# Attention with the rows of the next pair of heads made in the units in front, and three smaller moves around it

## The chip, the cores and the metric

The kernel runs on one core of a Trainium2 chip. The metric is the device time of one execution in microseconds (us). A core has a matrix engine (PE, whose weight loads are listed apart as PEld), three engines for elementwise work (DVE, ACT and POOL), and queues from which DMA transfers are issued (SP, ACT and POOL have one each).

## The reference

Two transformer blocks on 512 tokens of width 1024, in fp32. The first block ends in a mixture of 8 experts, of which each token takes two. The second block is the one that the change touches:

```python
    hn = modulate(rms_norm(h, norm1_g), shift1, scale1)
    qa, ka, va, qb, kb, vb = split(hn @ w_in)
    # a heads (8): dilated windows over rms-normalised q and k, added up with softmax weights
    for window, dilation in DILATED_PATTERNS:
        o, l = dilated_window_attention(rms_norm(qa), rms_norm(ka), va, table_a, window, dilation)
    # b heads (4): softmax(q1 k1 + bias) - lam * softmax(q2 k2 + bias), times v, rms-normalised
    o_b = differential_attention(qb[0], qb[1], kb[0], kb[1], vb, table_b, lam)
    h = h + gate1 * (concatenate([o_a, o_b]) @ w_out)
    hn = modulate(rms_norm(h, norm2_g), shift2, scale2)
    u = depthwise_conv_centred(hn @ w_up, conv_w, conv_b)      # 3 taps over tokens
    val, gate = split(u)
    h = h + gate2 * ((silu(gate) * val) @ w_down)
```

## The kernel before

Tokens lie in four blocks of 128 (`tb`). A product in fp32 is made of three matmuls (`mm3`, L173): each operand is split by `part` into a high part (a CAST on ACT, L167) and a low part (a subtraction on DVE, L168). Sums go to a pool of 8 banks of PSUM, tag `mm`. A scheduler of the framework puts the instructions of each engine in order when the kernel is built; `issue_after` makes an instruction stand behind another on the same queue. `skewed(units, lags)` runs generators one behind the other, each a step at a time.

**Combine.** Behind the last expert its rows `yde` are written to memory (L1582, issued on ACT's queue). Eight gathers on POOL's queue (L2236) fetch each token's two rows back. Per token block DVE adds them to `xres` (L2243) and takes statistics; POOL makes the factors of a layer norm from them (`bnrs`, L1137 to L1139), ACT applies these (`rsq`, L1140), DVE multiplies (L2247) and POOL adds a row vector (L2248). An RMS norm follows: ACT's squares (L2055), POOL's `rms` and `rrs`, and `rdg` on DVE (L2060), a diagonal matrix by which PE turns `xres` into the features `hT` (L1164, then `u` on ACT and DVE, L1169 and L1171). `gate3` and `gate4` are vectors that a DMA of POOL's queue spreads over all partitions (`bcast`, L301, tile `bc`, 512 KB each); they are wanted behind `w_out` and at the end.

**w_in.** Six column chunks (`ch`); in each, four pieces of weights of 256 rows, and with a piece six matmuls for each of the four token blocks.

**Attention.** `heads` makes the rows of a pair of a heads, or of a b head: PE transposes (L1890), then for each half six steps on ACT and DVE: three activations (L1899 to L1901) and two scaled subtractions (L1902, L1903), into `apair` or `act`. `zload` loads a head's bias rows and splits them (`zh`, `zl`). A unit is a quarter of a head's queries (`qb` 0 to 3). Its steps, in the lags (0, 1, 2, 4, 6): prepare; scores (four matmuls, L1918); maximum, exponential (`asc`, L1927), reciprocal and scaling (L1949, or L1975 for b heads); four transposes of the probabilities (L1935) and a copy to `PT` (L1936); the products with the values (L1960) at the last quarter of a pair. All of `heads` and `zload` is done in the prepare step of `qb` 0.

**Convolution.** For each pair of 128 columns of `w_up`, a value and a gate product of 24 matmuls over all 512 tokens each, then the taps, silu and product.

## Time and profile before

| | |
|---|---|
| median of 3 runs | 3006.85 us (3003.61 to 3007.26) |
| profiled execution | 2995.27 us, its span 2993.5 us |
| mean granted clock of PE | 0.906 |
| busy, share of the span | PE 88%, PEld 67%, DVE 57%, ACT 45%, POOL 27% |
| from the last expert to the first w_in product | about 2198 to 2253.5 us |
| w_in / attention / convolution FFN | to about 2385 / to about 2559 / from 2626.6 us |

The profile is one execution, some 0.4% below the median of the timed runs. A granted clock of 1.0 is 2.4 GHz, 0.5 is 1.2 GHz. In the rows further down, times are us from the start of the span; "out<-in" are the program's tile names; what stands in brackets is how long the engine had stood idle before the instruction, and whose end released it.

### The profile page before, as it was taken

The numbers are of one execution on the slowest core, as the hardware profiler recorded it, in microseconds if no ns is written. First come the engines' busy times: TensorE is split into PE (matmuls) and PEld (weight loads), VectorE is DVE, ScalarE is ACT, GpSimd is POOL, SyncE is SP. The second block draws the span as 40 slices with busy tenths as digits, with TensorE's granted clock in tenths as the row PEclk, the third lists the DMA queues.
The fourth block names the chain that finished last, engine by engine and source line by source line (L and its number), as shares of the span: only waits on it lengthen the run. The fifth ranks groups of instructions, "written<-read, shape, count | busy, mean of one in ns | idle before, by whom it ended". The sixth has DMA issues, their size and how long they took to land. (4 is left out here: it accounts for less than half of the span.)

```text
span 2993.5 us, 48068 instructions
## 1 busy us (share of the span) xinstructions
PE 2645.0 (88%) x18864; PEld 1998.6 (67%) x18864; DVE 1717.4 (57%) x2529; ACT 1335.1 (45%) x2338; POOL 822.6 (27%) x905
## 2 busy tenths in 40 slices
PE   6878798898898867789997999999949999899999
PEld 3666577677676556678776666455638756778887
DVE  5875656656756547664456423456675468554545
ACT  5644545645645433225442322345543367442422
POOL 2363435534525312016653300000042100102120
PEclk7986888987987978999998999999979989999999
DMA  7572334544544547666632877777762212223231
GB/s 259 175 235 69 97 116 131 177 153 129 168 122 117 156 147 236 203 198 212 198 120 101 286 277 274 262 259 267 279 212 81 62 42 70 71 71 99 98 97 58
DMA packets 301824, 477.92 MB, mean 160 GB/s; under 512 B 47283, under 2 KB 176068, under 8 KB 294936
## 3 DMA queue, kind: packets, MB, share of 16 engines
q1 hardware_dynamic: 283896, 404.81, 41.1%
q0 software_dynamic: 10480, 60.31, 6.1%
q10 hardware_dynamic: 7216, 9.68, 1.0%
q8 instruction: 151, 2.47, 0.3%
q14 instruction: 81, 0.66, 0.1%
HBM read 419.34 MB, written 55.39 MB: 159 GB/s over the span
## 5 line engine op out<-in xcount | busy, mean ns | idle before, releaser
L168 DVE TENSOR_TENSOR wl<-w,wh 128x1024 fp32r<-128x1024 f32 (+2 forms) x400 | 478.9, 1208 | 612.2 <-ACT wh L167 608.2
L167 ACT CAST wh<-w 128x1024 fp32r<-128x1024 f32 (+2 forms) x400 | 382.6, 966 | 619.4 <-PE mm L173 425.8
L173 PE MATMUL mm<-act,wh 128*128 128x512 f32 (+1 forms) x1440 | 446.1, 392 | 28.7 <-ACT act L167 22.8
L173 PEld LDWEIGHTS mm<-act,wh 128*128 128x128 f32 x1440 | 273.3, 193 | 87.5 <-ACT act L167 23.8
L173 PE MATMUL mm<-wh,act 128*128 128x512 f32 x884 | 288.1, 398 | 7.2 <-ACT wh L167 3.9
L173 PE MATMUL mm<-act,wl 128*128 128x512 f32 (+1 forms) x720 | 280.8, 390 | 4.8 <-DVE wl L168 4.8
L173 PEld LDWEIGHTS mm<-wh,act 128*128 128x128 f32 x884 | 168.1, 191 | 51.6 <-ACT wh L167 6.1
L173 PE MATMUL mm<-wl,act 128*128 128x512 f32 x474 | 188.9, 399 | 0.1
L286 POOL TENSOR_TENSOR act<-act 128x512 f32<-128x512 f32 x96 | 144.0, 1500 | 156.2 <-ACT act L285 141.5
L301 POOL DMA_DIRECT2D bc<-gate x6 | 3.5, 591 | 605.7 <-DVEq L1739 508.4
L173 PEld LDWEIGHTS mm<-act,wl 128*128 128x128 f32 x720 | 138.4, 192 | 35.0 <-DVE wl L168 7.7
L799 DVE STREAM_TRANSPOSE XT<-T 128x512 f16<-128x512 f16 x120 | 84.6, 705 | 99.3 <-ACT T L797 99.2
L743 POOL TENSOR_TENSOR GA<-GA,masks 128x512 f32<-128x512 f32 (+1 forms) x96 | 99.8, 1050 | 103.8 <-ACT GA L742 100.6
L739 PE MATMUL gm<-kr,bk 64*128 64x128 f32 (+1 forms) x768 | 117.1, 331 | 3.5 <-DVE kk L645 1.7
L792 DVE TENSOR_TENSOR W<-pW,masks 128x512 f16<-128x512 f32 x120 | 81.7, 681 | 65.9 <-PE pW L790 62.0
L285 ACT ACTIVATE act<-act,cT 128x512 f32<-128x512 f32 x96 | 68.4, 724 | 112.1 <-DMA act<-in_w_ada_dram 111.8
L739 PEld LDWEIGHTS gm<-kr,bk 64*128 64x128 f32 x768 | 101.2, 230 | 24.2 <-ACT GA L742 8.6
L173 PE MATMUL mm<-wh,moxl 128*128 128x512 f32 (+1 forms) x336 | 113.5, 381 | 0.3 <-ACT wh L167 0.3
L850 POOL TENSOR_TENSOR SP<-S,pc 128x64 f32<-128x64 f32 x176 | 59.0, 353 | 195.0 <-DVE S L890 183.6
L173 PE MATMUL mm<-wh,moxh 128*128 128x512 f32 (+1 forms) x336 | 107.0, 388 | 5.4 <-ACT wh L167 5.3
L173 PEld LDWEIGHTS mm<-wl,act 128*128 128x128 f32 x474 | 90.8, 192 | 28.3 <-issue 4.9
L288 DVE SCALAR_TENSOR_TENSOR act<-act,cT 128x512 f32<-128x512 f32 x96 | 74.2, 773 | 57.8 <-DMA act<-in_ada_w_dram 56.8
(529 smaller groups left out, 6155.8 us busy)
## 6 DMA issues: line engine op xcount, KB each, us to landing
w<-in_moe_w_dram SPq DMA_DIRECT2D x136, 512.0 KB
w<-in_moe_w_dram SPq DMA_DIRECT2D x40, 1024.0 KB
w<-in_ffn_w_dram SPq DMA_DIRECT2D x32, 1024.0 KB
act<-in_ada_w_dram SPq DMA_DIRECT2D x96, 256.0 KB
act<-in_w_ada_dram SPq DMA_DIRECT2D x96, 256.0 KB
w<-in_moe_w_dram SPq DMA_DIRECT2D x64, 384.0 KB
w<-in_w_up_dram SPq DMA_DIRECT2D x22, 1024.0 KB
x<-xdk POOLq DMA_DIRECT2D x18, 1024.0 KB, 6.0
```

Of the source, the lines that this page charges most:

```text
L167: self.nc.scalar.copy(out=hi, in_=x)
L168: self.nc.vector.tensor_tensor(out=lo, in0=x, in1=hi.bitcast(F32), op=OP.subtract)
L173: self.nc.tensor.matmul(ps, x, y, start=start and i == 0, stop=stop and i == 2, skip_group_check=True)
L285: nc.scalar.activation(out=wt, in_=wt, func=AF.Copy, scale=c)
L286: nc.gpsimd.tensor_tensor(out=acc, in0=wt, in1=acc if kk else bias, op=OP.add)
L288: nc.vector.scalar_tensor_tensor(out=acc, in0=wt, scalar=c, in1=acc if kk else bias, op0=OP.mult, op1=OP.add)
L301: (eng or self.nc.gpsimd).dma_start(out=t, in_=row_ap.to_broadcast([128, D]))
L739: nc.tensor.matmul(pss[par][:, s2, d, :nc_], bkj(d, par, j), KR[d][PR(par), j::12, :][:, :nc_ // 64, :], start=True, stop=True)
L743: nc.gpsimd.tensor_tensor(out=out, in0=out, in1=gm, op=OP.mult)
L792: nc.vector.tensor_tensor(out=W16, in0=pW, in1=lmask[:, li, None].to_broadcast(sh), op=OP.mult)
L799: nc.vector.transpose(fl(XT), fl(T16))
L850: nc.gpsimd.tensor_tensor(out=SP[:, d], in0=S[:, d], in1=PC[d][:, j:j + 1].to_broadcast([128, 64]), op=OP.mult)
```

## The change

Gate3's broadcast is put behind the last gather (`taken`) on POOL's queue. In w_in, chunk 0 takes its first three pieces of weights together, a token block at a time (18 matmuls in a row), and has three buffers of split weights instead of two. `heads` becomes a generator that gives its two halves one at a time; those of pair i+1 are made in the prepare steps of `qb` 1 and 2 of the last head of pair i, and a head's bias rows at `qb` 3 of the head in front. The first block of the convolution makes its value and gate products in halves of 256 tokens, value and gate of the first half ahead of the second half.

```diff
-            k.wq = win.enter_context(tc.tile_pool(reuse_waits="tile", name="wqC", bufs=2))
+            k.wq = win.enter_context(tc.tile_pool(reuse_waits="tile", name="wqC", bufs=3))
...
                         w = k.part(raw[:, 2 * q2:2 * q2 + 2, :])
+                        ws.append(w)
+                        if not ch and len(ws) < 3:
+                            continue
+
                         for tb in range(4):
-                            for k2 in range(2):
-                                kk = q * 4 + q2 * 2 + k2
+                            for kk in range(0 if len(ws) == 3 and not ch else 2 * len(ws) - 2, 2 * len(ws)):
+                                w, k2 = ws[kk // 2], kk % 2
                                 k.mm3(pss[tb], at(hT, ALL, kk, slice(tb * 128, (tb + 1) * 128)), at(w, ALL, k2), kk == 0, kk == KB - 1)
...
-        def heads(blk, hp):
+        def heads(blk, hp, out):
...
                 out.append((q, kh, kl, r))
-            return out
+                yield
...
+        order = [(0, hp) for hp in range(4)] + [(1, h) for h in range(4)]
+        coming = []
+
+        def start(i):
+            if i < len(order):
+                rowsets[order[i]] = []
+                coming.append(heads(*order[i], rowsets[order[i]]))
+
+        def prepare(i, h, qb, last):
+
+            if last and qb == 1:
+                start(i + 1)
+            if last and qb in (1, 2) and i + 1 < len(order):
+                next(coming[-1])
+            if qb == 3 and h < 11:
+                zs_[h + 1] = zload(h + 1)
+
+        start(0)
+        for _ in coming[0]:
+            pass
+        zs_[0] = zload(0)
 
         def unit_a(h, qb, st):
-            if qb == 0:
-                if h % 2 == 0:
-                    pairs[h // 2] = heads(0, h // 2)
-                st["hd"], st["z"] = pairs[h // 2][h % 2], zload(h)
-            yield
-            ps = scores(st["hd"], st["z"], qb)
+            prepare(h // 2, h, qb, h % 2 == 1)
+            yield
+            ps = scores(rowsets[0, h // 2][h % 2], zs_[h], qb)
...
         def unit_b(h, qb, st):
-            if qb == 0:
-                st["h1"], st["h2"] = heads(1, h)
-                st["z"] = zload(8 + h)
-            yield
-            pss = [scores(st[n_], st["z"], qb) for n_ in ("h1", "h2")]
+            prepare(4 + h, 8 + h, qb, True)
+            yield
+            pss = [scores(hd, zs_[8 + h], qb) for hd in rowsets[1, h]]
...
+        def products(ts, i, n=1):
+
+            ws = [k.part(t[:, :, i * 128:(i + 1) * 128]) for t in ts]
+            pss = [k.t(psp, [128, 512], tag="mm") for _ in ts]
+            for j in range(n):
+                cs = slice(j * NT // n, (j + 1) * NT // n)
+                for w, ps in zip(ws, pss):
+                    for kk in range(KB):
+                        k.mm3(ps[:, cs], at(w, ALL, kk), at(hT, ALL, kk, cs), kk == 0 and j == 0, kk == KB - 1 and j == n - 1)
+            return pss
...
-                    uv = conv(f + i, tv, i)
-                    ug = conv(22 + f + i, tg, i)
+                    if f + i:
+                        uv = conv(f + i, *products([tv], i))
+                        ug = conv(22 + f + i, *products([tg], i))
+                    else:
+
+                        pv, pg = products([tv, tg], i, 2)
+                        uv, ug = conv(f + i, pv), conv(22 + f + i, pg)
...
-                    nc.gpsimd.indirect_dma_start(out=got[c][:, tb, :], out_offset=None, in_=rows.yd,
+                    taken = nc.gpsimd.indirect_dma_start(out=got[c][:, tb, :], out_offset=None, in_=rows.yd,
...
-        gate3 = k.bcast(bc, k.gates["2"][0])
+        with tc.issue_after(taken.ins):
+            gate3 = k.bcast(bc, k.gates["2"][0])
```

On POOL, where the combine begins (`act_22171`, `act_22172` are the gathered rows, `bc_22383` is gate3, `bc_25357` gate4, `bnrs_22193` and `bnrs_22208` are the factors of token blocks 0 and 1), before (rows 652 to 656 are gathers like the two ahead of them):

```order
649 L301 DMA bc_25357<-gate_15617 128x1024
650 L2236 DMA act_22171<-yde,rt_rg 128x1024
651 L2236 DMA act_22172<-yde,rt_rg 128x1024
657 L2236 DMA act_22172<-yde,rt_rg 128x1024
658 L1137 TENSOR_SCALAR bnrs_22193<-bnag_22189 128x1
659 L1138 TENSOR_TENSOR bnrs_22193<-bnrs_22193,mhalf 128x1
660 L1139 TENSOR_TENSOR bnrs_22193<-bnrs_22193,bnnm_22191 128x1
661 L2248 TENSOR_TENSOR xres<-xres,bb_18774 128x1024
662 L1137 TENSOR_SCALAR bnrs_22208<-bnag_22204 128x1
663 L1138 TENSOR_TENSOR bnrs_22208<-bnrs_22208,mhalf 128x1
664 L1139 TENSOR_TENSOR bnrs_22208<-bnrs_22208,bnnm_22206 128x1
```

and now:

```order
654 L2269 DMA act_22171<-yde,rt_rg 128x1024
655 L2269 DMA act_22172<-yde,rt_rg 128x1024
656 L301 DMA bc_22383<-gate_15616 128x1024
657 L301 DMA bc_25357<-gate_15617 128x1024
658 L1137 TENSOR_SCALAR bnrs_22193<-bnag_22189 128x1
659 L1138 TENSOR_TENSOR bnrs_22193<-bnrs_22193,mhalf 128x1
660 L1139 TENSOR_TENSOR bnrs_22193<-bnrs_22193,bnnm_22191 128x1
661 L1137 TENSOR_SCALAR bnrs_22208<-bnag_22204 128x1
662 L1138 TENSOR_TENSOR bnrs_22208<-bnrs_22208,mhalf 128x1
663 L2281 TENSOR_TENSOR xres<-xres,bb_18774 128x1024
664 L1139 TENSOR_TENSOR bnrs_22208<-bnrs_22208,bnnm_22206 128x1
```

Both broadcasts stand behind the gathers now, ahead of the first `bnrs`; of block 1's three steps two have moved ahead of the add on `xres`.

On ACT, from the copy of the output of pair 0's products (`act_22387`) on, before (`apair` are the rows of a pair, `zh` a head's bias, `asc` the exponentials, `PT` the copies of transposed probabilities of the units that run):

```order
1800 L167 CAST act_22387<-mm_23580 128x512
1801 L1936 COPY PT_23554<-mm_23604 128x4x128
1802 L1936 COPY PT_23554<-mm_23623 128x4x128
1803 L1927 ACTIVATE asc_23662,asm_23663<-mm_23610,amx_23660 128x512
1804 L1899 ACTIVATE apair<-mm_23629,qncols 64x512
1805 L1900 ACTIVATE apair<-mm_23634,qncols 64x512
1806 L1901 ACTIVATE apair<-mm_23634,qncols 64x512
1807 L167 CAST zh_23734<-zr_23732 128x896
1808 L1936 COPY PT_23668<-mm_23669 128x4x128
1809 L1927 ACTIVATE asc_23682,asm_23683<-mm_23655,amx_23680 128x512
1810 L1936 COPY PT_23668<-mm_23688 128x4x128
1811 L1899 ACTIVATE apair<-mm_23629,qncols 64x512
```

and now, where the rows of the same pair (`apair<-mm_23561`, `mm_23566`) are made, up to that copy:

```order
1795 L1931 ACTIVATE asc_23548,asm_23549<-mm_23522,amx_23546 128x512
1796 L1931 ACTIVATE asc_23583,asm_23584<-mm_23541,amx_23581 128x512
1797 L1903 ACTIVATE apair<-mm_23561,qncols 64x512
1798 L1904 ACTIVATE apair<-mm_23566,qncols 64x512
1799 L1905 ACTIVATE apair<-mm_23566,qncols 64x512
1800 L1931 ACTIVATE asc_23618,asm_23619<-mm_23576,amx_23616 128x512
1801 L1903 ACTIVATE apair<-mm_23561,qncols 64x512
1802 L1904 ACTIVATE apair<-mm_23566,qncols 64x512
1803 L1905 ACTIVATE apair<-mm_23566,qncols 64x512
1804 L1940 COPY PT_23554<-mm_23555 128x4x128
1805 L1940 COPY PT_23554<-mm_23589 128x4x128
1806 L167 CAST act_22387<-mm_23595 128x512
```

These are the rows of pair 2. Its six activations stood behind the copy, in two groups with a bias between them; they now stand ahead of it, with one exponential between the groups, and the bias is elsewhere.

On PE, at the first products of the convolution, behind the last transposes (L1164), before (`mm_25377`, `mm_25410` are two sums over all 512 tokens):

```order
15329 L1164 MATMUL mm_25331<-rdg_25329,xres 128x128 x4
15330 L1164 MATMUL mm_25343<-rdg_25329,xres 128x128 x4
15331 L173 MATMUL mm_25377<-act_24961,wh_25378 128x512
15332 L173 MATMUL mm_25410<-act_24961,wh_25411 128x512
15333 L173 MATMUL mm_25447<-act_24961,wh_25448 128x512
15334 L173 MATMUL mm_25377<-act_24962,wh_25378 128x512
15335 L173 MATMUL mm_25377<-act_24961,wl_25379 128x512
```

and now (`mm_25385` is the value's sum, `mm_25386` the gate's):

```order
15311 L1164 MATMUL mm_25331<-rdg_25329,xres 128x128 x4
15312 L1164 MATMUL mm_25343<-rdg_25329,xres 128x128 x4
15313 L173 MATMUL mm_25385<-act_24961,wh_25377 128x256
15314 L173 MATMUL mm_25386<-act_24961,wh_25381 128x256
15315 L173 MATMUL mm_25385<-act_24962,wh_25377 128x256
15316 L173 MATMUL mm_25385<-act_24961,wl_25378 128x256
15317 L173 MATMUL mm_25385<-act_24961,wh_25377 128x256
15318 L173 MATMUL mm_25385<-act_24962,wh_25377 128x256
```

The matmuls have 256 columns, and of the features they need those of two token blocks first.

## Rows read from the trace of the kernel before

**Rows 1.** Busy times in stretches: w_in, attention, convolution FFN.

```profile
2260.00:2400.00 140.00, 134.42 (x587) 109.39 (x586) 61.41 (x91) 48.82 (x68) 29.00 (x16) 0.98 0.24 74
2400.00:2560.00 160.00, 146.27 (x683) 90.46 (x682) 118.36 (x271) 113.94 (x260) 11.59 (x16) 0.92 0.16 50
...
2660.00:2993.50 333.50, 328.56 (x1450) 271.83 (x1448) 158.33 (x190) 110.38 (x137) 49.96 (x36) 1.00 0.27 89
```

**Rows 2.** What PE waited for, 2230 to 2640: total us, times, longest.

```profile
PE mm L1164 <- DVE rdg L2060: 47.1, 4, 38.7
PE mm L1935 <- DVE asc L1949: 11.7, 4, 5.5
...
PE mm L1935 <- DVE asc L1975: 4.8, 5, 2.4
```

**Rows 3.** Timeline of ACT's queue and POOL behind the last expert: start, us, engine.

```profile
2198.92 2.89 ACTq L1582 DMA_DIRECT2D yde<-moo  x2
...
2200.18 0.65 POOL L301 DMA_DIRECT2D bc<-gate  x1 [508.43 <-DVEq L1739]
2207.98 1.04 POOL L2236 DMA_INDIRECT act<-yde,rt_rg  x1 [7.14 <-DMA yde<-moo]
...
2224.66 3.31 POOL L2248 TENSOR_TENSOR xres<-xres,bb 128x1024 f32<-128x1024 f32 x1 [2.89 <-DVE xres L2247]
...
2229.88 0.19 POOL L1139 TENSOR_TENSOR bnrs<-bnrs,bnnm 128x1 f32<-128x1 f32 x1
```

**Rows 4.** DMA issues, 2190 to 2300: queue, count, KB each, us to landing.

```profile
bc<-gate POOLq DMA_DIRECT2D x1, 512.0 KB, 4.9
```

**Rows 5.** Timeline of DVE at the end of the combine.

```profile
2237.96 4.51 DVE L168 TENSOR_TENSOR wl<-w,wh 128x1024 fp32r<-128x1024 f32 x2
...
2244.05 2.35 DVE L2060 TENSOR_SCALAR rdg<-ctile,rrs 128x128 f32<-128x128 f32 x1
```

**Rows 6.** Timeline of PE: combine, a pair of heads, the convolution's start.

```profile
2246.55 7.22 PE L1164 MATMUL mm<-rdg,xres 128*128 128x128 f32 x48 [5.43 <-DVE rdg L2060]
...
2434.70 1.09 PE L1935 MATMUL mm<-ctile,asc 128*128 128x128 f32 x4 [2.18 <-DVE asc L1949]
...
2626.61 2.07 PE L173 MATMUL mm<-act,wh 128*128 128x512 f32 x4 [6.16 <-ACT act L167]
```

**Rows 7.** Timeline of ACT in the pair that begins near 2427.

```profile
2426.89 0.67 ACT L1899 ACTIVATE apair<-mm,qncols 64x512 fp32r<-64x512 f32 x1
...
2446.28 0.69 ACT L1927 ACTIVATE asc<-mm,amx 128x512 f32<-128x512 f32 x1 [3.84 <-DVE amx L1924]
```

**Rows 8.** Stretches by clock: one, sum of four, one pair, its end, 2492, convolution.

```profile
2434.30:2444.50 10.20, 9.80 (x24) 5.43 (x25) 6.15 (x15) 4.86 (x12) 0.00 (x0) 0.50 0.08 23
...
2492.30:2495.70 3.40, 3.40 (x10) 2.12 (x9) 3.30 (x7) 2.66 (x6) 0.00 (x0) 0.50 0.18 35
...
sum 23.80, PE 23.40 PEld 13.00 DVE 17.31 ACT 12.98 POOL 0.00; mean PE 5.85 PEld 3.25 DVE 4.33 ACT 3.24 POOL 0.00
...
2434.70:2460.30 25.60, 23.44 (x88) 12.91 (x89) 15.62 (x32) 16.09 (x34) 0.00 (x0) 0.81 0.12 37
...
2445.00:2460.00 15.00, 13.14 (x64) 7.36 (x63) 9.58 (x17) 11.32 (x22) 0.00 (x0) 1.00 0.12 38
...
2625.40:2632.20 6.80, 5.59 (x13) 4.44 (x14) 2.20 (x5) 1.61 (x4) 0.00 (x0) 0.50 0.01 2
```

**Rows 9.** Timeline of DVE: low parts of the features ahead of the convolution.

```profile
2619.93 1.29 DVE L168 TENSOR_TENSOR act<-u,act 128x512 fp32r<-128x512 f32 x2
...
2626.58 1.29 DVE L168 TENSOR_TENSOR act<-u,act 128x512 fp32r<-128x512 f32 x2
```

**Rows 10.** Timeline of PE in the first block, products of 256 columns.

```profile
73.15 0.28 PE L173 MATMUL mm<-x,kh 128*128 128x256 f32 x1
...
73.63 0.28 PE L173 MATMUL mm<-x,kl 128*128 128x256 f32 x1
```

**Rows 11.** Weight loads of that stretch: count, ns minimum/median/maximum.

```profile
L173 PEld LDWEIGHTS mm<-s,lh x8: 186/188/190, 59.8 to 64.6; 128*128 128x128 f32 x8
```

More of the change, by code (lines that the diff above doesn't have):

```diff
@@ L1846, in phase_attn @@
                 pss = [k.t(psp, [128, 512], tag="mm") for _ in TB]
+                ws = []
                 for q in range(2):
@@ L1894, in heads @@
             npair[0] += 1
-            out = []
             for o in range(2):
@@ L1936, in transpose_p @@
             nc.scalar.copy(out=PT[:, :, qb * 128:(qb + 1) * 128], in_=pt)
-        pts, pairs = {}, {}
+        pts, rowsets, zs_ = {}, {}, {}
+        order = [(0, hp) for hp in range(4)] + [(1, h) for h in range(4)]
[15 more added lines that the diff above has]
+        zs_[0] = zload(0)
         def unit_a(h, qb, st):
-            if qb == 0:
-                if h % 2 == 0:
-                    pairs[h // 2] = heads(0, h // 2)
-                st["hd"], st["z"] = pairs[h // 2][h % 2], zload(h)
+            prepare(h // 2, h, qb, h % 2 == 1)
             yield
-            ps = scores(st["hd"], st["z"], qb)
+            ps = scores(rowsets[0, h // 2][h % 2], zs_[h], qb)
             yield
@@ L2013, in phase_convffn, with conv @@
         cw, cb = k.v3, k.v3["conv_b"]
-        def conv(f, t, i):
-            ps = k.t(psp, [128, 512], tag="mm")
-            w = k.part(t[:, :, i * 128:(i + 1) * 128])
-            for kk in range(KB):
-                k.mm3(ps, at(w, ALL, kk), at(hT, ALL, kk), kk == 0, kk == KB - 1)
+        def products(ts, i, n=1):
[7 more added lines that the diff above has]
+            return pss
+        def conv(f, ps):
             u = k.t(cs, [128, 512], tag="cu")
```

## The prediction

> **What bounds the kernel now.** I read the busy times by stage first [rows 1]; the columns are PE, PEld, DVE, ACT and POOL busy, then the clock. The w_in products (2260 to 2400) keep PE busy for 134.42 of 140 us and the convolution FFN (from 2660) for 328.56 of 333.5 us. These two are long rows of matmuls: when they start earlier they end earlier, and time saved ahead of them is not given back in them. The attention (2400 to 2560) has PE at 146.27 of 160 at clock 0.92, DVE at 118.36, ACT at 113.94: no engine is full there. Next I read what PE waited for [rows 2]. Between the last expert and the w_in products four waits for `rdg` come to 47.1 us; waits for the scaled probabilities `asc` come to 11.7 in the a heads (line L1949) and 4.8 in the b heads (L1975). A last place is the convolution's start, where PE waits 6.16 us for `act` [rows 6]. The change touches all of these.
>
> **Part 1, the gates.** Before, gate4's broadcast is issued at 2200.18 and the two writes of `yde` from 2198.92 to 2201.81; the first gather starts at 2207.98, after 7.14 us idle, released by `yde` [rows 3]. The broadcast took 4.9 us to land [rows 4], so until 2205.1. The change puts it and gate3's behind the eight gathers. If the second write began only when the broadcast was through, it now begins 2205.1 - 2201.8 = 3.3 us sooner; if the two went side by side at no loss, nothing is gained. I take 2.5, nearer to the upper end, because the gather came only 2.9 us after the broadcast's landing, about when a write that was held up by it would be in. In exchange two issues of 0.65 us (0.3 between them, an estimate from the pace of POOL's queue) now stand ahead of `bnrs` of block 0: 1.9 us. What counts on POOL is block 1. The add on `xres` of block 0 (3.31 us) stood ahead of all three `bnrs` of block 1, whose last ended at 2230.07 [rows 3]; now only the last, 0.19, follows it. That makes up for the 1.9 and leaves 0.5 better. So `rsq` of block 1 comes 0.5 + 2.5 = 3.0 earlier. From it depends `rdg` of block 1 (2244.05) [rows 5], and behind its transposes PE has no more wait up to the end of w_in. Gate3's broadcast hid nothing on the path where it stood before.
>
> **Part 2, the first w_in chunk.** The 48 transposes of blocks 1 to 3 take 7.22 us from 2246.55 [rows 6] and the products follow densely, so their order has nothing left to win. The third piece costs one CAST and one subtraction ahead of `u` and of `rdg` of block 2; two such subtractions took 4.51 us beside POOL's adds [rows 5], 2.3 each. PE has block 1's transposes meanwhile, which cover some of it. I charge 0.9, between nothing and 2.2. Parts 1 and 2: -3.0 + 0.9 = -2.1; ends -3.8 (3.3 and 0.5, no charge) and +1.7 (only the 0.5, and 2.2).
>
> **Part 3, attention.** Before, a pair's six activations (0.67 each), its bias and four DVE steps came in one lump ahead of the exponentials and copies of running units; PE then waited, as 2.18 us in pair 2 [rows 6]. In the same pair ACT stood idle for 3.84 us at another place [rows 7], because PE was at the values' products and the next scores came late. After each such wait PE runs at clock 0.50 for a while: 10.20 us in the worst case; over the four stretches it is busy for 23.40, of which half, 11.7, would not be there at full clock [rows 8]. Of the waits in [rows 2] the first and longest, 5.5, stands before any pair runs, and stays. That leaves 6.2 in the a heads. Their clock loss is 11.7 less the 1.7 of the stretch at 2492, so 10.0; together 16.2. The b heads' 4.8 and 1.7 make 6.5. The most that can be won is 22.7.
>
> Can PE be the bound afterwards? In the pair from 2434.7 to 2460.3 PE is busy for 23.44 [rows 8]; its clock loss is 9.80 / 2 = 4.9, so 18.5 at full clock. ACT has 16.09 and DVE 15.62: they fit, with 2.4 us to spare. The change hands the lump over in halves (2.0 us of ACT each) at the last head's units 1 and 2, next to the value products where ACT was idle, and the bias at unit 3. I leave 1.0 a pair, 3.0, since the halves still stand ahead of copies of PT. Of the b heads' 6.5 I take half, 3.2: their 16 units already fill PE nearly, and what remains may be their own waits. The first pair loses one activation, 0.7: it was done inside the last w_in piece and now stands ahead of the first scores. -16.2 + 3.0 - 3.2 + 0.7 = **-15.7**; ends -22.7 and -5 (a third: every pair keeps a wait, but a shorter one).
>
> **Part 4, convolution.** PE waits until 2626.61 for the features of the last block, and then runs at clock 0.50 for 5.59 busy microseconds, 2.8 lost [rows 6, 8]. Blocks 0 and 1 are whole at 2619.93 + 1.29 = 2621.2, the last at 2626.58 + 1.29 = 2627.9 [rows 9]. The change has 96 matmuls of 256 columns in place of 48 of 512. At full clock four of 256 start within 0.48 us, 0.12 each [rows 10]; 48 take 5.8. So the first half runs from 2621.0 to 2626.8, the second from about 2627.5 to 2633.3. Before, 48 of 512 at twice the 0.12 less a little (0.227) and the 2.8 brought the same work to 2626.6 + 10.9 + 2.8 = 2640.3. That is -7.0; half a microsecond for weights that come late: **-6.5**. If the whole first half stays at half clock, it takes 11.6, to 2632.6, and the rest to 2638.4: -1.9. Ends: -7.4 and -1.9.
>
> **Sum.** -2.1 - 15.7 - 6.5 = -24.3. The profiled execution took 2995.27, so 2971.0. It is 11.6 below the median of the runs, 3006.85, and I carry this over: **3006.85 - 24.3 = 2982.6**. A measurement of this kernel tells a change of about 0.2% (6 us) from none.
>
> **Rivals.**
> *The clock stays low.* The long waits go, but short gaps between units keep PE at 0.50. For it: the stretch of 10.20 us outlasts its wait by far, with matmuls all through it [rows 8]. Against: from 2445 to 2460 the same kinds of units run at clock 1.00 [rows 8]. It leaves the 11.7 lost: attention -(6.2 + 2.4 - 3.0 - 0.7) = -4.9, convolution -1.9, the rest -2.1: -8.9, 2998. The Trainium skill's page "TensorE: Matmul & The Clock Gate", section "A second HAM failure mode: psum-queue depth-cycling", says that short idles between groups of matmuls, as a kernel goes round the banks of PSUM, can throw the clock down again and again without any long wait. By that rule this rival wins; the trace shows clock 0.50 in the pairs only at and behind a wait of PE, and 1.00 between.
>
> *The stall only moves.* ACT still does all its work; the halves meet the copies of PT and each pair waits as long at another unit. Attention +0.7: -7.9, 2999.
>
> *Weight loads show.* The convolution's halves load every piece of the first weights twice. A load takes 0.188 us [rows 11]; were the 48 further ones not hidden, +9.0: the convolution would be at +2.5, the total at -15.3, 2991.6. The rows speak against it: starts 0.12 apart leave no room for 0.188 in line. The same page, section "The mechanism" of Part 3, says that a load runs beside a matmul only where the two use different row groups, which operands of 128 rows exclude (its section on the steps of a matmul in Part 2 names a background buffer as a second way); by the stricter sentence this rival holds, and the 0.12 differs from it.
>
> *Slower.* One mechanism: six activations with one exponential between them hold up the copies of PT, PSUM stays full, and PE stalls twice in each of seven pairs and b heads. At the worst price seen, 2.18 + 4.9 = 7.1 each, that is 49.7 against the 22.7 removed: +27.0 - 8.6 = +18.4, 3025. It comes out slower by 0.2% from (22.7 + 8.6 + 6) / 7 = 5.3 us each on. Against it stand ACT's 2.4 us to spare.
>
> **How the numbers follow.** Forecast (2975 to 2990): 0.65. Clock low: 0.12. Stall moves: 0.08. Weight loads: 0.02. All terms at their weak ends (-5 + 1.7 - 1.9 = -5.2), so within 0.2%: 0.08. Slower: 0.05. Faster by more than 0.2%: 0.87. The range takes in the three faster rivals: its high end is 3000, just above the moved stall; its low end is all terms at their best, -3.8 - 22.7 - 7.4 = -33.9, so 2973.
>
> **What would show it.** The first gather near 2205.5 and `rsq` of block 1 near 2227; in the attention no wait of PE for `asc` above 1 us between its first and the b heads, pairs of 18.5 to 19.5 us, clock near 1.00 in them; the group of 256-column matmuls done in about 12 us with no wait of 6 ahead of it. The prediction is wrong if PE waits for `asc` once a pair again, or if the clock in the pairs stays near 0.85.

## The result and the profile after

The changed kernel takes 2968.72 us (median of 4 runs, 2962.53 to 2975.09); the kernel before 3005.23 us (median of 4, 2993.93 to 3007.26). The ratio is 0.9899, with an interval of 0.9877 to 0.9921: 1.0% faster, some 30 us. Forecast were 24.3 us (0.8%). The median of 2968.72 lies 4 us under the lower end of the forecast's range (2973); the ratio applied to the 3006.85 that the forecast started from gives 2976.5, inside it. Why the two differ is told below: the first 2200 us of the program, which the change doesn't touch, take up to 24 us more or less from one execution to the next.

The profiled execution has a span of 2960.5 us, against 2993.5. First the busy times by stage, w_in, attention and convolution FFN (as in [rows 1]: PE, PEld, DVE, ACT, POOL busy, then the clock):

```profile
2249.80:2380.50 130.70, 130.70 (x579) 108.18 (x579) 56.55 (x84) 42.66 (x58) 26.07 (x16) 1.00 0.24 75
2381.30:2538.00 156.70, 142.75 (x714) 89.87 (x712) 126.55 (x290) 125.89 (x281) 10.48 (x16) 0.98 0.16 54
2594.70:2960.50 365.80, 360.74 (x1632) 299.82 (x1632) 178.75 (x219) 128.71 (x165) 52.54 (x38) 1.00 0.26 87
```

and the attention of the kernel before between the same two marks (first scores to the first product of w_out), which was not shown yet:

```profile
2385.60:2561.70 176.10, 155.16 (x714) 96.52 (x712) 127.16 (x289) 125.09 (x280) 11.59 (x16) 0.91 0.16 51
```

The attention went from 176.1 to 156.7 us. PE's busy time in it fell by 12.4 us though it does the same matmuls, at clock 0.98 in place of 0.91; the other 7.0 are waits. They are in the list of what PE waited for (total, times, longest; compare [rows 2]):

```profile
PE mm L1164 <- DVE rdg L2093: 44.7, 4, 36.1
PE mm L1939 <- DVE asc L1972: 5.9, 2, 4.8
PE mm L1939 <- DVE asc L1996: 3.5, 5, 1.5
...
PE mm L173 <- ACT act L167: 1.0, 2, 0.9
```

The waits for `asc` are 5.9 in two times in the a heads (11.7 in four before) and 3.5 in the b heads (4.8). The wait of 6.16 for `act` ahead of the convolution is 1.0. The four for `rdg` are 44.7 in place of 47.1.

PE's timeline at the places that the forecast spoke of (compare [rows 6]):

```profile
2232.29 3.79 PE L1164 MATMUL mm<-rdg,xres 128*128 128x128 f32 x16 [36.12 <-DVE rdg L2093]
2241.68 8.34 PE L1164 MATMUL mm<-rdg,xres 128*128 128x128 f32 x48 [5.61 <-DVE rdg L2093]
2249.78 0.48 PE L173 MATMUL mm<-wh,act 128*128 128x512 f32 x1
...
2390.25 1.11 PE L1939 MATMUL mm<-ctile,asc 128*128 128x128 f32 x4 [4.76 <-DVE asc L1972]
...
2404.62 0.66 PE L1939 MATMUL mm<-ctile,asc 128*128 128x128 f32 x4 [1.18 <-DVE asc L1972]
...
2594.72 0.51 PE L173 MATMUL mm<-act,wh 128*128 128x256 f32 x2 [0.85 <-ACT act L167]
...
2601.37 1.11 PE L173 MATMUL mm<-act,wh 128*128 128x256 f32 x4 [0.16 <-ACT act L167]
```

The last expert ends at 2232.29 - 36.12 = 2196.17. The attention's first wait is 4.76 us, a second of 1.18 comes in the first pair, and then none until the b heads. The pairs that follow last 18.3 us each with PE full:

```profile
2404.60:2422.90 18.30, 18.28 (x88) 10.44 (x88) 14.39 (x30) 15.51 (x32) 0.00 (x0) 1.00 0.20 56
2422.90:2441.20 18.30, 18.30 (x89) 10.44 (x88) 15.22 (x31) 16.01 (x34) 0.00 (x0) 1.00 0.16 53
```

What fills ACT now shows in the 16 products with the values of one pair. The first row is such a stretch in the changed kernel, the second one in the kernel before:

```profile
2411.20:2414.90 3.70, 3.70 (x18) 1.18 (x18) 3.49 (x7) 3.15 (x7) 0.00 (x0) 1.00 0.35 114
```

```profile
2441.80:2449.10 7.30, 7.30 (x22) 2.45 (x22) 3.09 (x8) 2.29 (x6) 0.00 (x0) 0.81 0.22 63
```

ACT was busy for 2.29 of 7.30 us there; now it is for 3.15 of 3.70, with the second half of the next pair's rows (activations at 2412.43, 2413.02 and 2413.70).

In the combine ACT's queue, ACT and POOL read thus (compare [rows 3]):

```profile
2196.48 2.82 ACTq L1582 DMA_DIRECT2D yde<-moo  x2
...
2225.14 1.24 ACT L1140 ACTIVATE rsq<-xres,bnrs 128x1024 f32<-128x1024 f32 x1 [7.06 <-DMA w<-in_w_in_dram]
...
2202.78 1.05 POOL L2269 DMA_INDIRECT act<-yde,rt_rg  x1 [513.51 <-DMA yde<-moo]
...
2214.03 1.19 POOL L301 DMA_DIRECT2D bc<-gate  x2
...
2221.29 2.33 POOL L2281 TENSOR_TENSOR xres<-xres,bb 128x1024 f32<-128x1024 f32 x1
2224.91 0.19 POOL L1139 TENSOR_TENSOR bnrs<-bnrs,bnnm 128x1 f32<-128x1 f32 x1 [1.29 <-DVE bnag L1133]
```

The first gather comes 6.3 us after the first write's issue (9.06 before), and the two broadcasts, 1.19 us together, stand behind the gathers.

To compare executions I cut each profile at marks on PE: end of the last expert, first transposes behind it, first product of w_in, first scores, first product of w_out, the products' first transposes ahead of the convolution, first product of the convolution, end. "Front" is all ahead of the first mark, "tail" all behind it. Each number is a difference of two such marks in PE's timeline (for the kernel before 2198.6, 2237.33, 2253.52, 2385.56, 2561.74, 2609.18, 2626.61 and 2993.5).

| kernel | front | to transposes | to w_in | w_in | attention | w_out | to conv | conv to end | tail |
|---|---|---|---|---|---|---|---|---|---|
| before | 2198.6 | 38.7 | 16.2 | 132.0 | 176.2 | 47.4 | 17.4 | 366.9 | 794.9 |
| changed | 2196.2 | 36.1 | 17.5 | 131.5 | 156.8 | 46.2 | 10.5 | 365.8 | 764.3 |
| e1_gates | 2208.8 | 36.6 | 15.9 | 132.0 | 177.7 | 46.4 | 17.4 | 366.3 | 792.3 |
| e2_win | 2220.1 | 38.4 | 16.8 | 131.5 | 173.7 | 47.6 | 17.2 | 367.1 | 792.2 |
| e3_attn | 2196.8 | 38.7 | 16.3 | 132.1 | 157.9 | 46.3 | 17.1 | 366.4 | 774.9 |
| e4_conv | 2208.3 | 38.8 | 16.6 | 132.0 | 175.0 | 46.4 | 10.8 | 366.1 | 785.8 |
| e5_rows | 2210.6 | 38.7 | 16.7 | 132.1 | 158.2 | 46.4 | 17.1 | 366.6 | 775.7 |
| e6_bias | 2207.7 | 39.0 | 16.1 | 132.1 | 176.2 | 47.4 | 17.4 | 366.9 | 795.2 |
| e7_lump | 2204.6 | 38.7 | 16.4 | 132.0 | 158.0 | 46.4 | 17.2 | 366.6 | 775.3 |
| e8_halves | 2197.3 | 36.8 | 17.4 | 131.5 | 156.7 | 46.3 | 10.5 | 378.5 | 777.6 |
| e9_far | 2211.4 | 39.1 | 15.9 | 132.9 | 164.0 | 46.2 | 17.4 | 366.2 | 781.7 |
| e10_gates_last | 2210.4 | 35.9 | 19.9 | 131.5 | 157.6 | 46.4 | 10.5 | 365.8 | 767.6 |
| e11_table | 2204.5 | 36.2 | 16.3 | 131.5 | 156.0 | 47.5 | 11.0 | 365.5 | 763.9 |
| e12_both | 2206.0 | 36.4 | 19.7 | 131.5 | 156.9 | 46.3 | 10.5 | 365.7 | 767.1 |

"To transposes" is the stretch from the last expert to the first transposes, "to w_in" from these to the first product of w_in, "to conv" from the transposes ahead of the convolution to its first product. From before to changed the tail lost 30.6 us: 2.6 + (-1.3) + 0.5 + 19.4 + 1.2 + 6.9 + 1.1, with roundings. The front lost 2.4 by chance.

### The profile page after: what moved, and what is told of

It reads as the page before. It is cut to its first block, busy times and chain, and to the rows that moved or that the text cites. A ratio compares the mean times of both kernels' runs of the same rounds, so it can differ in the third digit from the quotient of the medians.

```text
span 2960.5 us, 48159 instructions
## 1 busy us (share of the span) xinstructions
PE 2627.4 (89%) x18912; PEld 1993.3 (67%) x18912; DVE 1713.7 (58%) x2529; ACT 1334.8 (45%) x2338; POOL 822.4 (28%) x905
## 5 line engine op out<-in xcount | busy, mean ns | idle before, releaser
L173 PEld LDWEIGHTS mm<-act,wl 128*128 128x128 f32 x736 | 141.5, 192 | 30.6 <-DVE wl L168 3.8
L2269 POOL DMA_INDIRECT act<-yde,rt_rg x8 | 9.1, 1138 | 515.6 <-DMA yde<-moo 513.5
L797 ACT CAST T<-pT 128x512 f16<-128x512 f32 x120 | 69.6, 580 | 83.3 <-PE pT L795 80.1
```

The lines of the kernel that those rows point to most:

```text
L173: self.nc.tensor.matmul(ps, x, y, start=start and i == 0, stop=stop and i == 2, skip_group_check=True)
L797: nc.scalar.copy(out=T16, in_=pT)
L2269: taken = nc.gpsimd.indirect_dma_start(out=got[c][:, tb, :], out_offset=None, in_=rows.yd, in_offset=bass.IndirectOffsetOnAxis(ap=rt.rg[:, ...
```

## The experiments

**One part at a time.** Each of these is the kernel before with one part of the diff and nothing else.

*e1_gates*, the two broadcasts behind the gathers:

```diff
-        gate3 = k.bcast(bc, k.gates["2"][0])
+        with tc.issue_after(taken.ins):
+            gate3 = k.bcast(bc, k.gates["2"][0])
```

> The kernel before with the two broadcasts behind the gathers alone. Theory (the broadcast of 512 KB held up the second write of yde, and half of the gain is paid by two issues ahead of the factors of block 0): the first gather comes 6.3 us after the first write's issue in place of 9.1, rsq of block 1 2.5 us earlier counted from that issue, the first w_in product 2 to 3 us earlier, and the same again at the end: time -2 to -3 us. Rival (the write was not held up, and the gather came earlier in the changed kernel for another reason): gather 9.1 us after the issue, time unchanged or 1 us longer.

Measured in 12 runs against 32 of the kernel before: ratio 0.9996 (0.9976 to 1.0016), which cannot tell 2 us. The timelines of ACT, POOL and PE can:

```profile
2209.09 2.92 ACTq L1582 DMA_DIRECT2D yde<-moo  x2
...
2238.03 1.24 ACT L1140 ACTIVATE rsq<-xres,bnrs 128x1024 f32<-128x1024 f32 x1 [7.06 <-POOL bnrs L1139]
...
2215.70 1.05 POOL L2236 DMA_INDIRECT act<-yde,rt_rg  x1 [516.81 <-DMA yde<-moo]
...
2245.37 3.78 PE L1164 MATMUL mm<-rdg,xres 128*128 128x128 f32 x16 [36.59 <-DVE rdg L2060]
...
2261.28 0.48 PE L173 MATMUL mm<-wh,act 128*128 128x512 f32 x1
```

The gather comes 6.6 us after the write's issue (9.06 before), `rsq` of block 1 after 28.9 (31.2), the first product after 52.2 (54.6): 2.4 us earlier. The same shows in every profile: in the eight kernels with a broadcast issued ahead of the gathers the first gather comes 8.7 to 9.2 us after the write's issue, in the six without 6.1 to 6.8. The theory holds as far as the broadcast delayed the write; whether the write waited for it or the two shared the DMA engines, these rows do not tell. The tail is 2.6 shorter, since 1.5 more in the attention and 1.7 less in w_out and the convolution cancel. That its attention differs by 1.5 from the kernel before, with the same order of instructions, is taken up with e2.

*e2_win*, the first w_in chunk by token blocks (the first two pieces of the diff that stands with the change).

> The kernel before with the first w_in chunk by token blocks alone. Theory (PE is full from the transposes of block 1 on, so the order of the products wins nothing, and the third piece's subtraction delays those transposes): first product 1.1 us later after the first transposes of block 1 than in the kernel before (8.1 in place of 7.0 us), the rows of w_in products about 1.2 us shorter, sum 0 within 0.5 us. Rival (the products wait for features of blocks 1 to 3 in the kernel before, in gaps too short to be listed): w_in ends 2 us or more earlier.

Measured in 12 runs: ratio 1.0000 (0.9984 to 1.0016). PE:

```profile
2267.69 7.84 PE L1164 MATMUL mm<-rdg,xres 128*128 128x128 f32 x48 [5.40 <-DVE rdg L2065]
2275.29 0.47 PE L173 MATMUL mm<-wh,act 128*128 128x512 f32 x1
```

The transposes of blocks 1 to 3 take 7.84 us in place of 7.22, the first product comes 7.6 behind their start in place of 7.0, w_in is 0.5 shorter: up to the attention 186.7 us against 186.9. Nothing was won, nothing lost, as the theory has it; of its two terms each was half as large. In the attention this execution has 173.7 us, 2.5 less than the kernel before. Its waits for `asc` come to the same (11.6 and 4.8), though the first is 4.8 in place of 5.5 and the next three are longer (2.18, 2.48 and 2.18 for 1.80, 2.18 and 2.18); the order of the attention's first steps on ACT and DVE came out differently. Its row, and one stretch of it behind the last of these waits:

```profile
2406.80:2580.40 173.60, 152.70 (x714) 95.03 (x712) 128.01 (x290) 125.50 (x281) 11.61 (x16) 0.92 0.15 49
...
2482.00:2486.00 4.00, 3.92 (x20) 2.54 (x20) 3.83 (x9) 3.65 (x10) 0.00 (x0) 1.00 0.00 0
```

PE is busy for 152.70 where the kernel before has 155.16: the difference is in the clock, which stayed at 1.00 behind that last wait of 2.18 us. Executions with exactly the order of before in the attention (before, e1, e4, e6) have 175.0 to 177.7. PE stands idle for 21.0 to 21.2 us in all four and is busy for 153.9 to 156.6: the same waits leave more or less time at half clock. With early rows it is 156.7 to 158.2 in seven (156.0 in e11 and 164.0 in e9, further down).

*e3_attn*, early rows and biases:

> The kernel before with the attention's part alone. Theory (lumps of six activations ahead of the exponentials made PE wait once a pair, and the clock fell behind each wait): pairs of 18.3 us at clock 1.00, attention from its first product to the first of w_out 157 to 158 us in place of 176.3, time -18 to -20 us, of which w_out gains another 1.3 or nothing. Rival (the attention gained in part from what came before it, the earlier w_in or the third buffer of split weights): attention at 162 us or more.

Measured in 7 runs: ratio 0.9939 (0.9920 to 0.9959), some 18 us; tail 20.0 us shorter, attention 157.9, w_out 46.3. What PE waited for:

```profile
PE mm L1934 <- DVE asc L1967: 6.8, 2, 5.5
PE mm L1934 <- DVE asc L1991: 3.4, 5, 1.5
```

The same two and five waits as in the changed kernel, the first 5.5 in place of 4.8. The theory holds; the attention's gain needs none of the other parts but for 0.8 in that first wait, which is 4.8 in e2 as well and so comes with part 2.

*e4_conv*, the first block of the convolution in halves:

> The kernel before with the convolution's halves alone. Theory (PE waits for the features of the last block with those of two blocks at hand): the first product comes 10.5 us after the first transposes of that stage in place of 17.4, and clock 1.00 from there on: time -7 to -8 us. Rival (the clock stays at 0.50 behind the transposes, as it did behind the wait of 1.97 us there): -3 to -5 us.

Measured in 10 runs: ratio 0.9985 (0.9963 to 1.0007), which alone could be no change; tail 9.1 us shorter, of which 6.6 "to conv" and 0.8 behind it. PE:

```profile
2628.01 0.50 PE L173 MATMUL mm<-act,wh 128*128 128x256 f32 x2 [1.14 <-ACT act L167]
...
2634.66 1.11 PE L173 MATMUL mm<-act,wh 128*128 128x256 f32 x4 [0.16 <-ACT act L167]
```

Two waits of 1.14 and 0.22 us, 0.16 ahead of the second half, and no fall of the clock. The theory holds.

The four parts by themselves give 2.6 + 2.7 + 20.0 + 9.1 = 34.4 in the tail, all together 30.6; the differences lie in the spread of the attention and of w_out, and taken by their own stretches (2.4, 0.2, 18.3, 7.4) they give 28.3.

**What in the attention's part does it.** *e5_rows* leaves each bias at its own first quarter, *e6_bias* a pair's rows at theirs, and *e7_lump* makes both halves at the second quarter; their edits to the attention's part alone, in this order:

```diff
-            if qb == 3 and h < 11:
-                zs_[h + 1] = zload(h + 1)
+            if qb == 0 and h:
+                zs_[h] = zload(h)
```

```diff
-            if last and qb == 1:
-                start(i + 1)
-            if last and qb in (1, 2) and i + 1 < len(order):
-                next(coming[-1])
+            if i and qb == 0 and h == (2 * i if i < 4 else i + 4):
+                start(i)
+                for _ in coming[-1]:
+                    pass
```

```diff
-            if last and qb in (1, 2) and i + 1 < len(order):
-                next(coming[-1])
+            if last and qb == 1 and i + 1 < len(order):
+                for _ in coming[-1]:
+                    pass
```

> The kernel before with the rows of the next pair made early, but each head's bias still prepared at its own first quarter. All numbers are of the stretch from the first attention product to the first of w_out (176.2 us before, 157.9 with the attention's part alone). Theory (the six activations and four subtractions are the lump; a bias is one step of 0.95 us on ACT and 1.08 on DVE, which the units in flight cover): 157 to 160 us. Rival (the bias stands ahead of the scores that need it and PE waits for it at each head): 12 heads at 0.5 to 1 us and the clock behind, 165 us or more.

> The kernel before with only the bias prepared early, the rows of a pair in one lump at its first quarter. Same stretch. Theory (the lump of rows makes the stalls): one wait for the scaled probabilities in each pair stays, shorter by the bias's 0.95 us, with the clock's fall behind it: 168 to 175 us. Rival (the bias was the step that tipped it over): 162 us or less.

> The attention's part, but with both halves of a pair's rows at the second quarter of the last head, not one each at the second and the third. Same stretch. Theory (what counts is that the rows are made while PE is at the values' products, where ACT was idle; six activations of 0.68 in a row are hidden there too): 157 to 160 us. Rival (the split is what removes the wait; in one row of 4.1 us the activations hold up exponentials and copies of PT again): a wait of about 1 us or more in each pair, 163 us or more.

Measured: 158.2, 176.2 and 158.0 us. These numbers stand for less than the expectations supposed. In the attention the order of ACT, DVE and PE in e5 and e7 is that of e3, instruction for instruction, and in e6 that of the kernel before: the scheduler puts biases and halves where buffers and readiness let them go, whatever quarter they are written in. So moving the biases and dividing the rows do nothing here; of the attention's part, writing `heads` ahead of the seam is all that works. Whether a bias in another place on ACT would cost or bring time, and whether six activations in one row would, these runs do not tell. They are repeats: two executions of the old order with 176.2, three of the new with 157.9 to 158.2.

*e9_far* does move the rows to another place: to the second and third quarter of the first head of a pair, some 9 us earlier.

```diff
         def prepare(i, h, qb, last):
 
+            last = h % 2 == 0 if i < 4 else last
             if last and qb == 1:
                 start(i + 1)
```

> The attention's part, but in the a heads the rows of the next pair are made at the second and third quarter of the first head of a pair, away from the values' products; b heads as in the attention's part. Stretch from the first attention product to the first of w_out, 157.9 us with the attention's part. Theory (as the prediction put it: the six activations are free because they fall beside the values' products, where ACT was idle): ACT is late elsewhere, waits of about 1 us or more for the scaled probabilities in each of three pairs with the clock behind, 163 us or more. Rival (it is enough that the rows are there before the seam of two pairs; ACT has 2.4 us to spare in a pair and the units in flight cover the rest): pairs of 18.3 us, 157 to 160 us.

Measured: 164.0 us. PE waited for

```profile
PE mm L1934 <- DVE asc L1968: 7.9, 1, 7.9
PE mm L1934 <- DVE arc L1928: 4.2, 3, 1.4
```

and two of its pairs, then the stretch that begins 1.6 us behind the third of these waits, read

```profile
2429.50:2449.20 19.70, 18.34 (x88) 10.40 (x88) 15.33 (x31) 16.07 (x34) 0.00 (x0) 1.00 0.15 48
2449.20:2469.00 19.80, 18.37 (x89) 10.47 (x89) 15.42 (x32) 16.16 (x34) 0.00 (x0) 1.00 0.16 48
...
2470.60:2474.00 3.40, 3.40 (x11) 1.46 (x12) 3.09 (x8) 1.67 (x6) 0.00 (x0) 0.52 0.47 135
```

Three waits of 1.4 in three pairs: 19.75 us a pair in place of 18.3, PE's work unchanged. The first wait grew as well, from 5.5 to 7.9, since the rows of pair 1 now come into the start; e3's second wait, of 1.2, is gone. That makes 4.2 + 2.4 - 1.2 = 5.4 us of the 6.1 by which it is slower than e3. The place matters: beside the values' products the rows are free, a head earlier they are not, though ACT has the same 16.1 of 19.7 us to do. The expectation had the clock fall behind each of these waits. It stayed at 1.00 behind the first two and fell to its lower level behind the third, for some 3.4 us, of which half, 1.7, was lost; w_in, 0.8 longer than in e3, took over a part of the attention's work.

**The convolution's weight loads.** *e8_halves* is the changed kernel with all products of the convolution in halves:

```diff
-                        uv = conv(f + i, *products([tv], i))
-                        ug = conv(22 + f + i, *products([tg], i))
+                        uv = conv(f + i, *products([tv], i, 2))
+                        ug = conv(22 + f + i, *products([tg], i, 2))
```

> The changed kernel with every product of the convolution in halves of 256 tokens, not the first block alone: 42 further products, each with 24 further weight loads. Counted from the convolution's first product to the end, 361.1 us in the changed kernel. Theory (a load hides beside a matmul of 256 columns; a half costs 0.12 in place of 0.227 / 2): +0.3 a product, +13 us, 374. Rival (the further loads show, 0.188 each): +190 us.

Measured: 378.5 from the first product to the end against 365.8, +12.7. (The expectation's 361.1 runs to the end of PE's last product; counted so, this kernel has 373.8.) The weight loads of this kernel in that stretch, then busy times in it and in the changed kernel:

```profile
2640.00:2970.00 330.00, 330.00 (x2283) 309.26 (x2281) 151.98 (x182) 105.76 (x131) 48.70 (x35) 1.00 0.26 85
```

```profile
L173 PEld LDWEIGHTS mm<-act,wh x896: 187/192/192, 2732.4 to 2937.1; 128*128 128x128 f32 x180
```

```profile
2640.00:2955.00 315.00, 315.00 (x1392) 260.82 (x1390) 150.38 (x179) 105.82 (x131) 48.67 (x35) 1.00 0.27 89
```

A load is listed with 0.192 us and PEld is busy for 309 of 330 us, yet PE has no gap: here loads hide beside matmuls of 256 columns. The rival is out, and with it the stricter sentence in Part 3, section "The mechanism", of the Trainium skill's "TensorE: Matmul & The Clock Gate"; its background buffer is what these rows agree with.

**Attempts at more.** All three are the changed kernel with an edit. *e10_gates_last* puts the broadcasts behind the last of the four adds on `xres` (L2281, kept in a list `adds`); *e11_table* adds an exponential on one column of zeros behind w_in's last square; *e12_both* has both.

```diff
-        with tc.issue_after(taken.ins):
+        with tc.issue_after(adds[-1].ins):
```

```diff
+                    if ch == 4 and tb == 3:
+                        nc.scalar.activation(out=one, in_=sq[:, 0, 0:1], func=AF.Exp, scale=0.0)
```

> The changed kernel with the two broadcasts behind the last add on the token rows, 30 us later on POOL's queue; in the order that results, the add of block 0 stands ahead of block 1's factors again. Theory (two issues, 1.2 us, delay only block 0's factors; the add of 2.3 to 3.3 us ahead of block 1's factors costs more): the stretch from the last expert to the first transposes grows from 36.1 to 36.6 or more. Rival (the two issues and their 1 MB beside the gathers are what is left of the cost): 35.5 us or less.

Measured: 35.9 us to the first transposes, between the two; but 19.9 from there to the first product in place of 17.5, and 3.3 us more in the tail. POOL and PE of e10_gates_last:

```profile
2255.36 1.26 POOL L301 DMA_DIRECT2D bc<-gate  x2
...
2259.08 0.19 POOL L2089 TENSOR_SCALAR rms<-rms 128x1 f32<-128x1 f32 x1 [2.20 <-ACT rsq L2088]
2259.35 1.49 POOL L2091 TENSOR_TENSOR rrs<-rms,mhalf 128x1 f32<-128x1 f32 x2
```

```profile
2246.39 3.78 PE L1164 MATMUL mm<-rdg,xres 128*128 128x128 f32 x16 [35.94 <-DVE rdg L2093]
...
2261.09 5.44 PE L1164 MATMUL mm<-rdg,xres 128*128 128x128 f32 x32 [2.03 <-ACT u L1169]
2266.28 0.48 PE L173 MATMUL mm<-wh,act 128*128 128x512 f32 x1
```

With the 1.2 us of issues gone from the front and the add back ahead of block 1's factors, the two cancel. The issues now stand ahead of `rms` of block 2, and the order on POOL came out differently behind them: `rrs` of blocks 2 and 3 stand in a row (x2 at 2259.35), so that block 2's stands behind a wait of 2.20 us for ACT's square of block 3. PE waits 2.03 us in the middle of its transposes. So the new order, and not only the 1.26 us of issues, costs time here; the attention's order on ACT and DVE changed too. Neither case of the expectation looked there.

> The changed kernel with one more ACT step, an exponential of one column on zeros, behind the last square in w_in, so that the table of the exponential is loaded there. Theory (the load of 1.28 us stands in the chain of the first four exponentials while PE waits): the first wait of the attention falls from 4.76 to about 3.5 us, the attention from 156.8 to about 155.5. Rival (the chain hangs on DVE's maxima of the first scores, not on ACT): 156.5 or more.

Measured: the first wait is 4.52 us, not 3.5, and the attention 156.0. ACT, DVE and PE:

```profile
2367.58 1.28 ACT L1878 ACT_TABLE_LOAD   x1
...
2393.66 1.88 DVE L1931 TENSOR_REDUCE amx<-mm 128x1 f32<-128x512 f32 x3
2395.58 0.76 DVE L1910 SCALAR_TENSOR_TENSOR apair<-mm,qncols,apair 64x512 fp32r<-64x512 f32 x1
...
2397.11 1.12 PE L1942 MATMUL mm<-ctile,asc 128*128 128x128 f32 x4 [4.52 <-DVE asc L1975]
```

The table's load is out of the chain, at 2367.58, and the four exponentials are done 0.9 us earlier behind the first scores. But DVE's three maxima and a subtraction, to 2396.34, stand ahead of the reciprocals and the scaling that PE waits for, so 0.24 us are left of 1.28. The rival is the better description, though the attention came out half a microsecond under its 156.5. The tail, 763.9 against 764.3, is no difference that these runs can tell.

> The changed kernel with both of these, the broadcasts last and the table early. If both theories of the two hold: 0.5 us slower in front, 1.3 faster in the attention, -0.8 us in all against the changed kernel; 0.989 of the kernel before. Rival (both rivals): -0.6 in front and 0 in the attention.

Measured in 4 runs against 7 of the kernel before: ratio 0.9892 (0.9851 to 0.9933), tail 767.1, which is 2.8 us more than the changed kernel's: the loss of e10 and nothing to set against it. No version here beats the changed kernel beyond doubt.

## Why the prediction was right

It forecast faster by 24.3 us; measured are 30.6 us in the tail of the two profiles, and 1.0% (0.8 to 1.2) in the timed runs. The four mechanisms are as described, but for half a microsecond of part 1. The sizes are less good: 3.7 of the 6.3 us that were missing are part 3's, 1.5 part 4's, and some 1.2 a chance of w_out's clock. Each by itself:

- **Part 1, gates: -3.0 forecast, -2.4 by e1.** The write was held up: the gather came 2.5 to 2.8 us earlier (2.5 taken). The further 0.5 had no row behind it: block 1's three steps ended 2.1 us behind the add (2227.97 to 2230.07), of which 0.2 stay, so the move wins 1.9, just the charge. That the two issues took 1.19 in place of 1.9 brought nothing either, since DVE became the last to be ready on block 1's path. This is the changed kernel:

```profile
2221.69 3.02 DVE L2276 SCALAR_TENSOR_TENSOR xres<-act,rt_g,xres 128x1024 f32<-128x1024 f32 x1
2224.63 0.14 DVE L1135 TENSOR_SCALAR bnnm<-bnag 128x1 f32<-128x1 f32 x1
```

  An add that takes 1.27 us elsewhere took 3.02 beside POOL's add, and `bnnm`, which POOL's last step needs, stood behind it.
- **Part 2, w_in: +0.9 forecast, 0 by e2 alone.** In the changed kernel the transposes take 8.34 in place of 7.22, and 0.5 comes back within w_in. The charge was right in place and too high by about half. Together parts 1 and 2 were put at -2.1, and the changed kernel reaches its first scores 1.9 us earlier from the last expert (185.1 against 186.9).
- **Part 3, attention: -15.7 forecast, -19.4 measured, -18.3 alone.** This term makes most of the error. I left 1.0 us a pair, 3.0 in all, for waits that the halves might still make; there is one of 1.18 in the first pair (against the sign that none above 1 us would come there), and none in the others. And I charged 0.7 to the start, where the wait fell from 5.51 to 4.76 (by part 2) and its time at half clock from 4.73 to 3.40 busy microseconds:

```profile
2390.30:2393.70 3.40, 3.40 (x14) 3.23 (x15) 1.87 (x5) 1.86 (x3) 0.00 (x0) 0.50 0.00 0
2594.70:2607.00 12.30, 11.90 (x92) 11.18 (x93) 7.01 (x14) 6.72 (x14) 0.00 (x0) 1.00 0.01 2
```

  (The first row is that stretch, the second the convolution's first 12 us.) In all, 7.0 of the 19.4 are waits (5.0 in the a heads behind the first, 0.75 in the first, 1.3 in the b heads), the rest is clock. The b heads' -3.2 was right: 1.3 of waits and 1.7 of clock. That pairs would last 18.5 by PE alone, by its busy time less half of the stretch at clock 0.50, came out at 18.3.
- **Part 4, convolution: -6.5 forecast, -8.0 measured (-6.9 to its first product, -1.1 behind it), beyond the best end, -7.4.** The forecast let the first product wait until the low parts of blocks 0 and 1 were whole, 11.8 us behind the transposes (2621.0 - 2609.18). It came after 10.5: the first products take the high parts, and PE then waited 0.22 for a low one. The half microsecond for late weights was not needed. The first half took 2594.72 to 2601.2, 6.5 in place of 5.8, the second started at 2601.37 with 0.16 of wait; the clock stayed at 1.00, so the 2.8 of lost clock are gone too. e8 shows a half's price right (12.7 against 13).
- **w_out, not in the forecast: -1.2.** It has 47.4 to 47.6 in four executions and 46.2 to 46.4 in ten, in both orders of the attention. In all 14 PE waits 2.4 us ahead of it and then runs at clock 0.50, in the four for some 6.8 us (5.66 busy in the kernel before, 2560.6 to 2567.4), in the ten for some 3.4 (2.96 in the changed kernel, 2537.6 to 2541.0). Half of the difference is 1.35. So this gain is one of clock. Both values come with either order of the attention (47.5 with early rows in e11, 46.4 without them in e1 and e4), so the change alone does not decide it, and I count it as luck.

Of the rivals, the clock that stays low is out: 1.00 through the pairs and the convolution. That a stall only moves was out for the place chosen; e9 shows that it would have happened a head earlier, and costs 1.4 us a pair, and once the clock behind it. Weight loads are out by e8. The stalls twice a pair did not come. Of what the Trainium skill's page "TensorE: Matmul & The Clock Gate" says in "A second HAM failure mode: psum-queue depth-cycling" nothing shows in the changed kernel's pairs, which stay at clock 1.00; in e9 the clock fell behind one of three waits of 1.4 us.

## What to carry to other kernels

Work that feeds the next group of units belongs beside the stretch where its engine stands idle, and that stretch can be read from the timeline; e9 had the same work on the same engines, with room for it, and lost a third of the attention's gain by the place. PE's busy time less half of what it spent at half clock tells what a stage can come down to, and that bound was reached within about 1% (18.5 forecast, 18.3 measured). Where a front that nobody touched varies by more than the change is worth, cut profiles at marks of the program and compare the stretches.

## What was not expected of the hardware

The front, the same instructions in every kernel here, took 2196.2 to 2220.1 us in 14 executions, while the tails of kernels with one order agree within 1 us (774.9, 775.7 and 775.3; 794.9 and 795.2), though the attention by itself spreads over 2.7 us in four executions of the old order. The spread of the timed runs, 2982.57 to 3008.55 for the kernel before in 32 runs, is of that size. Between the shortest and the longest it is PE's clock: for the same 15664 matmuls PE is busy for 1927.6 us at clock 0.89 in the changed kernel and for 1953.7 at 0.88 in e2. In others the waits differ as well (e3 has PE busy for 1935.9 of 2196.8). Where in the front it arises was not followed up.

The length of a wait did not decide whether PE's clock fell. Behind two waits of 1.40 us in e9 it stayed at 1.00, behind a third of 1.39 it fell to 0.50; at the waits of 2.18 us in the kernel before it fell, behind one of 2.18 in e2 it did not. How long it then stays low also varies between executions of one order, and this, not the waits, is the spread of the attention and of w_out.

A step of DVE on 128x1024 elements took 1.27 us with POOL at no add and 3.02 with POOL at an add of the same size; POOL's add took 2.33 in that company and 3.31 in another.
